# Two SBUF pools, another ring for the split branch outputs, and new transfer times in the instruction planner of a two-layer hybrid decoder

## The chip, the cores and the metric

The kernel runs on one core of a Trainium2 chip. The metric is the device time of one execution in microseconds (us), where less is better. Three runs of the kernel before gave 2449.2, 2452.07 and 2451.95 us, so the median is 2451.95 us.

A core has five engines that run their own instruction streams in order and meet through semaphores: TensorE (PE in the profile, with its weight loads shown apart as PEld), VectorE (DVE), ScalarE (ACT), GpSimd (POOL), and SyncE (SP), which here issues every transfer between HBM and SBUF.

## The reference

The reference is a trunk of two layers over 1024 tokens of width 1024, batch 1, in float32. Each layer does the following.

```python
mod = c_act @ w_ada + b_ada                    # shift, scale, gate per channel
h = rms_norm(x, norm_g) * (1.0 + scale) + shift
proj = h @ w_in                                # one projection, 8,320 columns
o_pool = causal_pool_mixer(pool_u, ...) * silu(pool_g)
o_ret  = retention(q, k, v, ...) * silu(ret_g)
o_rwkv = rwkv7_time_mix(rw, ...) * silu(rw_g)
y = einsum('btnw,nwd->btnd', branches, w_branch)
x = x + gate * (sum(sigmoid(gate_logits) * y, axis=branch) @ w_out)
```

After the second layer a final RMSNorm is applied. The pooling mixer takes trailing windows of 2 to 16 tokens, retention works in chunks of 128 tokens with 4 heads, and the RWKV-7 mixer has 8 heads of 64 with a state that is carried from token to token.

## The kernel before, in words

The activations lie transposed, channels on the 128 partitions and 512 tokens (half `h` of 0 and 1) along the free dimension. Every large product is done in `float32r` with both operands split in two, a high part that float32r holds and a low remainder, so one product of a 128x128 block takes three matmuls (`mm1`, L909): high weights with high activations, high weights with low activations, low weights with high activations. The weights are loaded in tiles of 128x512 (`wr`), and `split` (L922) makes `wh` from them on ACT and `wl` on POOL. The normed activations are `hhi` and `hlo`, 32 tiles of the ring `hb`. The outputs of the three branches go through DRAM (`od`), come back as `ol`, and are split by `split_o` (L1821) into `oG` (high) and `olo` (low); `olo` comes from the ring `mi`, eight tiles of 528 elements. The gate values, which were computed early, are kept in DRAM (`gd`) and come back into tiles of the list `gs_free` (L1841), first the seven of the ring `ri` and the four of `rk`.

The kernel does not issue its instructions where they are written. `Prog.record` (L274) notes each operation with the views it writes and reads, and gives it the priority of a running clock that the code around it keeps. `slots` (L287) gives each tile a place in its ring, `needs` (L308) finds the dependences, `cost` (L344) gives each operation a duration and a time for which it occupies its engine, and `weave` (L403) is a list scheduler: again and again it takes the engine that can start something first, and there the startable operation of the lowest priority number, until the order of every engine's stream is fixed. `give` (L458) then hands the operations to the real engines in that order, and gives each ring place its SBUF tile, all from one pool `sb`, one behind the other in the order of first use. The times of `cost` reach the chip only as this order. What an engine really waits for are the semaphores of the dependences, and an instruction whose inputs are late holds up everything behind it in its stream.

For a transfer, `cost` books 50 ns of SP and 2700 ns until it has landed, whatever else is under way; the expression in `weave` that looks at `lanes` (L424) always yields zero. VectorE and GpSimd operations with two large inputs are marked with `lock`, and `weave` does not let a locked operation of the one run beside a locked one of the other.

The program starts with the setup of layer 0 (from L1644): the eight tiles of `x` for half 0 are loaded, then the constants and the parameter vectors of layer 0 (`vec0`), four tiles of `w_ada` (into `ringG`), eight tiles of `x` for half 1, and weights. VectorE sums the squares and computes the shifts and scales in six groups (`ada`, L607) as weighted sums over `w_ada` tiles. The first large matmuls of the layer (`mms`, L1614, weights `wbig`, sums `acc6`) need the normed, shifted and split tile of each of the eight channel blocks, and the groups give the shifts of one to two blocks each. The parameter vectors of layer 1 (`vec1`) are loaded at the end of the task `rope_tables` (L694), and `derive(1)` (L695) turns them with four small VectorE operations.

Each layer then walks through its list of projection columns, with the mixers' tasks pumped in between, until ("merge",), and after it through gates, branch products and output products.

Of the kernel before, what the change touches and what calls it, by code (L numbers as in the profile page):

```python
# [10 lines left out]
F32R = mybir.dt.float32r  # L11
# [7 lines left out]
P = 128  # L19
# [239 lines left out]
class Prog:  # L259
# [14 lines left out]
    def record(self, eng, name, what, args, kw):  # L274
        o = Op()
        o.eng, o.what, o.args, o.kw = eng, (name, what), args, kw
        out = kw["out"] if "out" in kw else args[0]
        o.outs = [out]
        o.ins = [x for x in list(args) + list(kw.values()) if isinstance(x, View) and x is not out]
        o.i = len(self.ops)  # L280
        o.lane = self.lane[0]
        o.prio = self.now()
        o.pred, o.succ = {}, []
        self.ops.append(o)
        return o

    def slots(self):  # L287
        for o in self.ops:
            for x in o.outs + o.ins:
                b = x.tensor  # L290
                if b.first is None:
                    b.first = o.i
                b.last = o.i
        self.chains = {}
        used, turn = {}, {}
        for b in sorted((b for b in self.bufs if b.first is not None), key=lambda b: b.first):
            ends = used.setdefault(b.key, [])
            if len(ends) < b.bufs:
                ends.append(-1)
                k = len(ends) - 1  # L300
            else:
                k = min(range(b.bufs), key=lambda j: ends[j])
            turn[b.key] = k
            ends[k] = b.last
            b.slot = (b.key, k)
            self.chains.setdefault(b.slot, []).append(b)
# [37 lines left out]
    def cost(self, o):  # L344
        n = max((x.free_size() for x in o.outs + o.ins if x.index is not None), default=512)
        psum = any(x.space == PSUM for x in o.ins)
        wide = [x for x in o.ins if x.index is not None and x.free_size() == n and x.free_size() > 1]
        w = o.what[1]
        o.lock, o.table = False, 0
        if o.eng == "PE":  # L350
            n = o.outs[0].free_size()
            rhs = o.ins[1]
            k = rhs.index.shape[0] * 32
            if rhs.dtype == F32R:
                o.occ, o.dur = ((n + 32) / 2.4, n / 2.4 + 176) if k == 128 else (116, 393)
            elif w == "transpose":
                o.occ, o.dur = 108, 272
            elif k == 128:
                o.occ, o.dur = 222, 386 if n > 1 else 361
            else:  # L360
                o.occ, o.dur = (111, 278) if k == 64 else (64, 223)
            return
        if o.eng == "SP":
            o.occ, o.dur = 50, 2700
            return
        if o.eng == "DVE":
            if w == "reciprocal":
                d = 140 + 6.2 * n
            elif w == "transpose":
                d = 100 + 1.82 * n  # L370
            elif w == "tensor_tensor_scan":
                d = 150 + 1.7 * n
            elif w == "tensor_reduce":
                d = 150 + 1.04 * n
            elif w == "memset":
                d = 60 + 0.8 * n
            elif psum or o.outs[0].space == PSUM:
                d = 160 + 1.03 * n
            elif len(wide) > 1 or w == "tensor_tensor":
                d, o.lock = 150 + 1.05 * n, True  # L380
            else:
                d, o.lock = 150 + 0.53 * n, True
            o.dur, o.occ = d, d - 80
        elif o.eng == "ACT":
            d = (150 if psum else 185) + 0.84 * n
            if w == "activation":
                f = o.args[2] if len(o.args) > 2 else o.kw.get("func")
                o.table = SETS.get(getattr(f, "name", str(f)).split(".")[-1], 0)
                d += 100 * isinstance(o.kw.get("scale"), View) + 90 * isinstance(o.kw.get("bias"), View)
            o.dur, o.occ = d, d - 104  # L390
        else:
            if w == "memset":
                d = 100 + 0.83 * n
            elif w == "tensor_copy":
                d = 180 + 1.0 * n
            elif o.kw.get("op") == ALU.pow:
                d = 370 + 158 * n
            else:
                thin = any(0 in x.index.strides[-1:] for x in o.ins)
                d, o.lock = 190 + (1.66 if n > HF or thin else 2.12) * n, True  # L400
            o.dur, o.occ = d, d - 55

    def weave(self):  # L403
        ops = self.ops
        for o in ops:
            self.cost(o)
            o.est, o.left = 0.0, len(o.pred)
        free = {e: 0.0 for e in SPACE_LAT}
        lock = {"DVE": 0.0, "POOL": 0.0}
        ready = {e: [] for e in free}  # L410
        for o in ops:
            if not o.left:
                ready[o.eng].append(o)
        lanes, table = [0.0] * 8, 0
        order = []
        other = {"DVE": "POOL", "POOL": "DVE"}
        while len(order) < len(ops):
            best = None
            for e, q in ready.items():
                if not q:  # L420
                    continue
                f = free[e]
                if e == "SP":
                    f = max(f, lanes[len([1 for x in order if 0]) % 8])  # L424
                lk = lock[other[e]] - 100 if e in other else 0.0
                t = min(max(f, o.est, lk if o.lock else 0.0) for o in q)
                if best is None or t < best[0]:
                    best = (t, e, f, lk)
            t, e, f, lk = best
            lim = t + 1e-6 + (30 if e == "PE" else 0)  # L430
            q = ready[e]
            o = min((o for o in q if max(f, o.est, lk if o.lock else 0.0) <= lim), key=lambda o: (o.prio, o.i))
            q.remove(o)
            s = max(f, o.est, lk if o.lock else 0.0)
            d, c = o.dur, o.occ
            if o.table and o.table != table:
                d, c, table = d + 1283, c + 1283, o.table
            o.start, o.end = s, s + d
            free[e] = s + c
            if o.lock and e in lock:  # L440
                lock[e] = o.end
            order.append(o)
            for i in o.succ:
                p = ops[i]
                kind = p.pred[o.i]
                if p.eng != e or e == "SP":
                    r = o.end + SPACE_LAT[p.eng]
                elif kind == "d" and e != "PE":
                    r = o.end + SPACE_LAT[e]
                else:  # L450
                    r = s
                p.est = max(p.est, r)
                p.left -= 1
                if not p.left:
                    ready[p.eng].append(p)
        return order

    def give(self, ctx, tc):  # L458
        nc = tc.nc
        sb = ctx.enter_context(tc.tile_pool(name="sb", bufs=1))  # L460
        ps = ctx.enter_context(tc.tile_pool(name="ps", bufs=1, space=PSUM))
        dr = ctx.enter_context(tc.tile_pool(name="dr", bufs=1, space=DRAM))

        def real(b):
            if b.real is None:
                tag = "_".join(b.key) + str(b.slot[1])
                if b.space == DRAM:
                    b.real = dr.tile(b.shape, b.dtype, name=b.name)
                    return b.real
                w = HF if b.space == PSUM else self.width[b.key]  # L470
                r = (ps if b.space == PSUM else sb).tile([P, w], b.dtype, tag=tag, name=b.name)
                n = 1
                for x in b.shape[1:]:
                    n *= x
                if n != w:
                    r = r[:, 0:n]
                if len(b.shape) == 3:
                    r = r.rearrange("p (a b) -> p a b", b=b.shape[2])
                b.real = r
            return b.real  # L480
# [10 lines left out]
def trunk_kernel(ctx, tc, xT, cvec, pos, vecs, consts, w_ada, w_all, pool_w, lora_w, out):  # L491
# [1286 lines left out]
    for l in range(L):  # L1778
# [41 lines left out]

        def split_o(G, row, kt, o, h):  # L1821
            hi = G[:, kt * T + h * HF : kt * T + (h + 1) * HF].bitcast(F32R)
            lo = mi("olo").bitcast(F32R)
            split(o, hi, lo)
            row.append((hi, lo))

# [11 lines left out]
                    split_o(G, row, kt, o, h)  # L1838
                    yield 1250

        gs_free = [t_ri] * 7 + [t_rk] * 4 + [t_vp] * 2 + [t_cs] * 2  # L1841
        gs_used = {}

        def gate_tile(key):
# [232 lines left out]
```

## Time and profile before

| | |
|---|---|
| median of three runs | 2451.95 us |
| the profiled execution | 2445.24 us |
| its span | 2443.2 us |
| PE busy | 2349.6 us, 96% of the span |
| PE weight loads busy | 1903.0 us, 78% |
| VectorE, ScalarE, GpSimd busy | 1423.0, 857.1 and 845.6 us |
| transfers, mean | 92 GB/s |
| granted TensorE clock | 0.996 |

The time of an execution is slightly over its span, which runs from the first to the last recorded instruction. Matmuls are pipelined and overlap in the record, so that a busy PE is not a PE at its peak; the number of matmuls or of weight loads in a stretch says more. The windows view gives, for a stretch of time, each engine's busy time and in brackets its number of instructions. The timeline gives start, duration, engine, line, operation and tiles, with the engine's idle time before it and what ended it.

All instructions have line 487 in the profile, since `give` issues them all; they are told apart by the names of their tiles.

### The profile page before, as it was taken

What the parts mean: (1) busy time and instruction counts of PE and PEld (TensorE: products, weight loads), DVE (VectorE), ACT (ScalarE), POOL (GpSimd) and SP (SyncE); (2) the same over time, 40 slices, a digit from 0 to 9 for tenths busy, and PEclk for the clock granted to TensorE, in tenths of its full rate; (3) what the DMA queues carried; (4) which work ended last, traced back from release to release, by engine and by line L of the source; (5) the groups of instructions that cost most, each with busy time, mean ns of one, the idle gap of its engine ahead of it and who ended that gap; (6) DMA issues with size and microseconds to landing.
All of it is one profiled execution on the core that took longest, in us unless ns stands there. A gap on an engine that the chain in (4) does not pass through costs nothing. (4 is left out here: it accounts for less than half of the span.)

```text
span 2443.2 us, 33796 instructions
## 1 busy us (share of the span) xinstructions
PE 2349.6 (96%) x12520; PEld 1903.0 (78%) x12520; DVE 1423.0 (58%) x2802; ACT 857.1 (35%) x1706; POOL 845.6 (35%) x738
## 2 busy tenths in 40 slices
PE   1999999999999999998999999999999999999998
PEld 1777878878887778777887887788788778877888
DVE  4677368567657843457555845854774784412343
ACT  3642433343333232212253334334333423321343
POOL 3322233243233323364452233323323333236441
PEclk9999999999999999999999999999999999999999
DMA  6232112111213223666631211211221122454252
GB/s 218 69 90 89 44 40 71 57 44 53 82 46 94 92 70 112 211 196 199 218 109 48 87 35 44 79 42 37 66 65 37 57 99 61 128 152 144 83 149 78
DMA packets 125364, 225.68 MB, mean 92 GB/s; under 512 B 14224, under 2 KB 17552, under 8 KB 125200
## 3 DMA queue, kind: packets, MB, share of 16 engines
q1 hardware_dynamic: 125200, 223.54, 29.8%
q8 instruction: 98, 1.61, 0.3%
q14 instruction: 66, 0.54, 0.1%
HBM read 175.51 MB, written 47.97 MB: 91 GB/s over the span
## 5 line engine op out<-in xcount | busy, mean ns | idle before, releaser
L487 PE MATMUL acc<-hlo,wh 128*128 128x512 f32 x2000 | 815.1, 408 | 0.0
L487 PE MATMUL acc<-hhi,wh 128*128 128x512 f32 x2000 | 811.6, 406 | 3.2 <-DVE silu L487 2.5
L487 POOL TENSOR_TENSOR wl<-wr,wh 128x512 fp32r<-128x512 f32 x342 | 457.0, 1337 | 1028.1 <-ACT wh L487 955.6
L487 PE MATMUL acc<-hhi,wl 128*128 128x512 f32 x2000 | 811.5, 406 | 0.0
L487 PEld LDWEIGHTS acc<-hhi,wh 128*128 128x128 f32 x2000 | 377.2, 189 | 76.4 <-DVE silu L487 2.8
L487 PEld LDWEIGHTS acc<-hlo,wh 128*128 128x128 f32 x2000 | 377.4, 189 | 73.8 <-issue 3.3
L487 PEld LDWEIGHTS acc<-hhi,wl 128*128 128x128 f32 x2000 | 377.2, 189 | 73.3 <-issue 2.2
L487 ACT CAST wh<-wr 128x512 fp32r<-128x512 f32 x342 | 211.6, 619 | 622.4 <-PE acc L487 422.5
L487 PE MATMUL acc<-oG,wh 128*128 128x512 f32 x384 | 152.6, 401 | 8.5 <-ACT oG L487 6.2
L487 PE MATMUL acc<-olo,wh 128*128 128x512 f32 x384 | 153.5, 400 | 7.0 <-POOL olo L487 6.6
L487 PE MATMUL acc<-oG,wl 128*128 128x512 f32 x384 | 151.6, 395 | 0.0
L487 ACT COPY xst<-Z 64x64 f32<-64x64 f32 x256 | 62.3, 243 | 176.8 <-DVE Z L487 173.8
L487 DVE SCALAR_TENSOR_TENSOR S<-ch,pc,SP 64x64 f32<-64x64 f32 x224 | 63.4, 283 | 89.1 <-PE ch L487 80.9
L487 DVE COPY xst<-cy 64x64 f32<-64x64 f32 x256 | 55.5, 217 | 93.1 <-PE cy L487 72.2
L487 DVE TENSOR_TENSOR tm<-VB 64x30 f32<-64x30 f32 (+14 forms) x240 | 102.8, 428 | 7.6
L487 DVE TENSOR_TENSOR VB<-VB,tm 64x30 f32<-64x30 f32 (+14 forms) x240 | 98.5, 410 | 7.2
L487 DVE COPY Z<-ch 64x128 f32<-64x128 f32 x128 | 36.1, 282 | 110.4 <-PE ch L487 110.1
L487 PEld LDWEIGHTS acc<-oG,wh 128*128 128x128 f32 x384 | 72.1, 189 | 30.8 <-ACT oG L487 11.7
L487 DVE SCALAR_TENSOR_TENSOR gs<-gs,acc 128x512 f32<-128x512 f32 x64 | 43.4, 685 | 90.0 <-PE acc L487 83.0
L487 PEld LDWEIGHTS acc<-olo,wh 128*128 128x128 f32 x384 | 72.5, 189 | 26.9 <-POOL olo L487 11.4
L487 PEld LDWEIGHTS acc<-oG,wl 128*128 128x128 f32 x384 | 72.6, 189 | 16.0
L487 ACT ACTIVATE SP<-S,pc 128x128 f32<-128x128 f32 x120 | 48.2, 401 | 79.8 <-DVE S L487 79.5
(269 smaller groups left out, 3718.7 us busy)
## 6 DMA issues: line engine op xcount, KB each, us to landing
wr<-in_w_all SPq DMA_DIRECT2D x364, 256.0 KB, 2.7
gd<-gsg SPq DMA_DIRECT2D x84, 256.0 KB, 2.0
gs<-gd SPq DMA_DIRECT2D x84, 256.0 KB, 2.8
wada<-in_w_ada SPq DMA_DIRECT2D x70, 256.0 KB, 3.4
ol<-od SPq DMA_DIRECT2D x64, 256.0 KB, 3.0
ringG<-in_w_ada SPq DMA_DIRECT2D x26, 256.0 KB, 4.7
x<-in_xT SPq DMA_DIRECT2D x16, 256.0 KB, 4.8
od<-po SPq DMA_DIRECT2D x16, 256.0 KB, 2.0
```

The source lines that it names most:

```text
L487: f(*[put(x) for x in o.args], **{k: put(x) for k, x in o.kw.items()})
```

## The change

The change has five parts.

1. `record` leaves the written view out of the inputs by its place in the call, where before it left out every input that was the same view. An operation in place, such as `x = x * r`, now counts `x` as an input too; the costs and the running clock see it.
2. `slots`: where all places of a ring are still in use when a tile is first used, the place whose tile began first is taken; before, it was the one whose tile ends first.
3. The costs: a transfer occupies SP for 470 ns and takes 2650 ns, or 2100 ns where it leaves SBUF; `weave` lets no transfer land sooner than 680 ns after the one before it, and starts none before the eighth last has landed. A scan on VectorE gets the lock. A VectorE operation on PSUM costs 150 + 1.04 ns per element, or 215 + 1.0 with two full inputs, where it was 160 + 1.03.
4. `give` opens a second pool `sa`, for all tiles whose width is a multiple of 128 elements (512 bytes); the others stay in `sb`.
5. `olo` takes its tiles from `ri` (seven) and `rk` (one), 512 elements wide; the loaded gates take the eight of `mi` and three of `rk` first.

```diff
     def record(self, eng, name, what, args, kw):
-        out = kw["out"] if "out" in kw else args[0]
+        rest = [v for k, v in kw.items() if k != "out"]
+        out, rest = (kw["out"], list(args) + rest) if "out" in kw else (args[0], list(args[1:]) + rest)
         o.outs = [out]
-        o.ins = [x for x in list(args) + list(kw.values()) if isinstance(x, View) and x is not out]
+        o.ins = [x for x in rest if isinstance(x, View)]
...
-                k = min(range(b.bufs), key=lambda j: ends[j])
+                k = min(range(b.bufs), key=lambda j: ends[j] if ends[j] < b.first else b.first + began[b.key, j])
+            began[b.key, k] = b.first
...
         if o.eng == "SP":
-            o.occ, o.dur = 50, 2700
+            o.occ, o.dur = 470, 2100 if o.ins[0].space != DRAM and o.ins[0].tensor.key else 2650
...
             elif w == "tensor_tensor_scan":
-                d = 150 + 1.7 * n
+                d, o.lock = 150 + 1.7 * n, True
...
             elif psum or o.outs[0].space == PSUM:
-                d = 160 + 1.03 * n
+                d = (215 + 1.0 * n) if len(wide) > 1 else 150 + 1.04 * n
...
-        lanes, table = [0.0] * 8, 0
+        landed, table = [0.0] * 8, 0
...
                 if e == "SP":
-                    f = max(f, lanes[len([1 for x in order if 0]) % 8])
+                    f = max(f, landed[-8])
...
+            if e == "SP":
+                o.end = max(o.end, landed[-1] + 680)
+                landed.append(o.end)
...
+        sa = ctx.enter_context(tc.tile_pool(name="sa", bufs=1))
...
-                r = (ps if b.space == PSUM else sb).tile([P, w], b.dtype, tag=tag, name=b.name)
+                r = (ps if b.space == PSUM else sb if w % P else sa).tile([P, w], b.dtype, tag=tag, name=b.name)
...
-            lo = mi("olo").bitcast(F32R)
+            lo = olo_ring[olo_n[0] % 8]("olo").bitcast(F32R)
+            olo_n[0] += 1
...
-        gs_free = [t_ri] * 7 + [t_rk] * 4 + [t_vp] * 2 + [t_cs] * 2
+        olo_ring, olo_n = [t_ri] * 7 + [t_rk], [0]
+        gs_free = [mi] * 8 + [t_rk] * 3 + [t_vp] * 2 + [t_cs] * 2
```

More of the change, by code (lines that the diff above doesn't have):

```diff
@@ L294, in slots @@
         self.chains = {}
-        used, turn = {}, {}
+        used, began = {}, {}
         for b in sorted((b for b in self.bufs if b.first is not None), key=lambda b: b.first):
@@ L301, in slots @@
             else:
-                k = min(range(b.bufs), key=lambda j: ends[j])
-            turn[b.key] = k
+                k = min(range(b.bufs), key=lambda j: ends[j] if ends[j] < b.first else b.first + began[b.key, j])
+            began[b.key, k] = b.first
             ends[k] = b.last
```

## The prediction, written before the result was known

> **What bounds the kernel now.** I read the page first, then the stretches of the first 80 us, then PE's and VectorE's timelines there, and last the long stretches of large matmuls.
>
> ```profile
> span 2443.2 us, 33796 instructions
> PE 2349.6 (96%) x12520; PEld 1903.0 (78%) x12520; DVE 1423.0 (58%) x2802; ACT 857.1 (35%) x1706; POOL 845.6 (35%) x738
> ...
> PE   1999999999999999998999999999999999999998
> ...
> PE acc L487 <- POOL olo L487: 6.6, 6, 2.8
> PE acc L487 <- ACT oG L487: 6.2, 7, 1.1
> PE rot L487 <- DVE yc L487: 6.1, 6, 2.4
> ```
>
> PE is full in every slice but the first, and from 80 us on the view of PE's waits has only a few entries of some us (the three largest stand here: us in all, times, longest). From there to the end PE's own matmuls set the time. A gain must come from PE's pace or from its start, and any us that PE's full stretch begins earlier is a us of the total.
>
> The start is another matter. The columns are length, then busy time and count of PE, PEld, DVE, ACT, POOL, then clock, DMA share and GB/s.
>
> ```profile
> 5.00:10.00 5.00, 0.00 (x0) 0.00 (x0) 0.00 (x0) 2.96 (x5) 0.00 (x0) 1.00 1.01 358
> 10.00:15.00 5.00, 0.00 (x0) 0.00 (x0) 0.70 (x6) 0.00 (x0) 0.00 (x0) 1.00 1.05 395
> 15.00:20.00 5.00, 0.00 (x0) 0.00 (x0) 0.00 (x0) 0.00 (x0) 0.00 (x0) 1.00 1.06 387
> 20.00:25.00 5.00, 0.00 (x0) 0.00 (x0) 0.00 (x0) 0.00 (x0) 0.00 (x0) 1.00 1.06 388
> 25.00:30.00 5.00, 0.00 (x0) 0.00 (x0) 2.71 (x10) 0.63 (x1) 0.00 (x0) 1.00 0.39 119
> 50.00:55.00 5.00, 2.72 (x8) 2.25 (x8) 4.43 (x10) 2.66 (x4) 4.94 (x7) 1.00 0.04 14
> 70.00:80.00 10.00, 10.00 (x44) 7.94 (x43) 9.82 (x14) 9.79 (x14) 7.08 (x6) 1.00 0.24 91
> ```
>
> From 10 to 25 us the data streams in at 387 to 395 GB/s and nobody works on it. The timelines say who waits for what:
>
> ```profile
> 6.14 2.57 ACT L487 ACTIVATE sq<-x 128x512 f32<-128x512 f32 x4 [0.70 <-DMA x<-in_xT]
> ...
> 10.24 0.17 DVE L487 TENSOR_SCALAR omu<-vec 128x13 f32<-128x13 f32 x1 [9.32 <-DMA vec<-in_vecs]
> 27.29 0.17 DVE L487 TENSOR_SCALAR omu<-vec 128x13 f32<-128x13 f32 x1 [16.32 <-DMA vec<-in_vecs]
> 28.38 0.68 DVE L487 TENSOR_TENSOR sq<-sq,sq 128x512 f32<-128x512 f32 x1
> 28.98 0.48 DVE L487 SCALAR_TENSOR_TENSOR ada_ps<-ringG,cact,ada_ps 128x256 f32<-128x256 f32 x1
> 49.29 2.48 DVE L487 TENSOR_TENSOR x<-x,rbc 128x512 f32<-128x512 f32 x4 [1.34 <-ACT rbs L487]
> 79.83 0.75 DVE L487 SCALAR_TENSOR_TENSOR ada_acc<-ringG,cact,ada_ps 128x512 f32<-128x512 f32 x1
> ...
> 50.88 2.07 PE L487 MATMUL acc<-hhi,wbig 128*128 128x512 f32 x4 [2.25 <-ACT hhi L487]
> 65.04 1.22 PE L487 MATMUL acc<-hhi,wbig 128*128 128x512 f32 x2 [1.41 <-ACT rn L487]
> 69.33 2.78 PE L487 MATMUL acc<-hhi,wbig 128*128 128x512 f32 x9
> ...
> 18.31 3.72 SPq L487 DMA_DIRECT2D wada<-in_w_ada  x6
> 22.37 0.33 SPq L487 DMA_DIRECT2D vec<-in_vecs  x1
> ```
>
> The second `omu` is the first instruction of `derive(1)`, for layer 1, which nobody needs for a thousand us. It stands in VectorE's stream ahead of the sums for layer 0, and its load is issued at 22.37 us behind the six `wada`. VectorE sits 16.32 us on it, after 9.32 us on `vec0`. The old costs book every landing 2.7 us after an issue that takes 50 ns, so in the plan `vec1` is there at once and its four small operations fill a hole. PE is full from 69.33 us on.
>
> **The change part by part.**
>
> *Transfer times (SP 470 ns, 680 ns between landings).* At 388 GB/s the 262,144 bytes of a tile take 676 ns, so the plan now follows the stretch of 10 to 25 us. `vec1`, some thirtieth in the queue, lands in the plan at about 30 x 0.68 + 2.65 = 23 us or later instead of at 4, and the VectorE work that is ready before that is placed ahead of `derive(1)`. The load itself can stay where it is: behind it on SP stand only ring loads that wait for VectorE. What can fill the two holes, by what has landed (bytes summed over the stretches: all of `x` half 0 by 8.7 us, where ACT's squares end; four `ringG` tiles by 12; half 1 by 17; the next four `ringG` by 22)? Seven adds for half 0, 7 x 0.68 = 4.8; group 0, 8 x 0.48 = 3.8; four adds for half 1, 2.7; two normings of 2.48 / 4 = 0.62, 1.2; group 1, 3.8. That is 16.3 us of VectorE's work done before 27.3 us. From 27.29 to 79.83 us, where the last group ends, VectorE is busy about 43 of 52.5 us (the stretches of which three stand above, summed with the others of that view), so 16.3 us less to do brings that end forward by 16.3 x 52.5 / 43 = 20 us, and PE's full stretch with it. Bounds: at worst the later groups meet the loads for the ring instead, since its eight places are refilled only as VectorE empties them. Seven such loads take 5.6 us each to land (row below); two rounds exposed cost 11, and 20 - 11 = 9. At best VectorE stalls no more at all: the 43 - 16.3 = 27 us after 27.3 end at 54, 25 us early. I take 20.
>
> ```profile
> ringG<-in_w_ada SPq DMA_DIRECT2D x7, 256.0 KB, 5.6
> ```
>
> Elsewhere the new times cost nothing: weight tiles are loaded three ahead, a tile feeds 24 matmuls or 24 x 0.233 = 5.6 us of PE, and GpSimd, which makes the low half, sits idle before each split, so the tile waits for a free place and not the place for the tile:
>
> ```profile
> L487 POOL TENSOR_TENSOR wl<-wr,wh 128x512 fp32r<-128x512 f32 x342 | 457.0, 1337 | 1028.1 <-ACT wh L487 955.6
> ```
>
> 1028.1 / 342 = 3.0 us each. If that cover were gone, each late tile would cost what it is late beyond 3 us.
>
> *Two pools.* The compiled program before places `wh` and `wl` at 80256 and on, 384 modulo 512, and thirty of the 32 `hhi`/`hlo` tiles at 416, because tiles of odd width lie between them; two `hb` tiles and all `oG` lie at 384. With all widths in `sa` multiples of 512 bytes, all of them agree. The trace holds both cases. Four long stretches of `hhi`/`hlo` matmuls, then four of `oG`/`olo`:
>
> ```profile
> 201.60:237.98 36.38, 36.38 (x157) 29.25 (x156) 34.14 (x67) 7.12 (x13) 8.23 (x7) 1.00 0.31 95
> 1372.00:1408.36 36.36, 36.36 (x157) 29.25 (x156) 33.28 (x69) 7.74 (x14) 9.75 (x8) 1.00 0.23 73
> 1577.42:1611.47 34.05, 34.05 (x147) 27.37 (x146) 30.61 (x66) 7.82 (x15) 8.08 (x9) 1.00 0.25 77
> 2117.83:2147.43 29.60, 29.60 (x128) 23.81 (x127) 4.44 (x5) 7.93 (x15) 12.43 (x10) 1.00 0.68 215
> 2157.03:2201.32 44.29, 44.29 (x192) 35.88 (x191) 10.31 (x15) 5.47 (x9) 10.33 (x8) 1.00 0.45 127
> 2213.98:2238.85 24.87, 24.87 (x109) 20.28 (x108) 6.62 (x10) 3.11 (x5) 20.28 (x16) 1.00 0.43 123
> 1051.17:1075.75 24.58, 24.58 (x107) 19.92 (x106) 13.13 (x21) 2.76 (x5) 21.36 (x16) 1.00 0.75 230
> 1129.60:1151.47 21.87, 21.87 (x96) 17.82 (x95) 21.70 (x33) 8.10 (x14) 6.45 (x7) 1.00 0.54 157
> ```
>
> By the count of weight loads, one to a matmul, the first four take 136.39 us / 585 = 233.1 ns and the others 115.61 / 500 = 231.2 ns. The 1.9 ns are not the neighbours' doing: VectorE is near full in two of the first four and idle in the fourth, with one pace. Three groups of 2000 matmuls with `hhi`/`hlo` stand on the page, so 6000 x 1.9 = 11.6 us, all on the path, as PE is the bound. Ends: the slowest `oG` stretch, 44.29 / 191 = 231.9, gives 6000 x 1.2 = 7; the fastest, 21.87 / 95 = 230.2, gives 17. I take 12, the mean with a little for the output products. The Trainium skill speaks against this: SBUF — State Buffer, section "Who interferes with whom", gives PE two independent read ports, one for the moving operand and one for LDWEIGHTS, and says that PE never waits on anyone. By that page the addresses are worth 0 and the time is that of rival B below; these rows show two paces, if only 0.8% apart, and cannot say why.
>
> *`olo` and the gates.* The same instructions on exchanged rings, eight places for `olo` as before and fifteen for gates. The new risk is that `ri` is still held by the last RWKV outputs when the first branch's `olo` wants it. That is hidden by gate matmuls that stand ready; if the cover goes, the price is the row of POOL's burst, once per layer: 0 to 10 us each. I take 0.
>
> ```profile
> 1115.32 10.42 POOL L487 TENSOR_TENSOR olo<-ol,oG 128x512 fp32r<-128x512 f32 x7
> ```
>
> *Compute costs, inputs in place, ring places.* They issue nothing new; they move instructions. Some come nearer to the rows and one goes further off:
>
> ```profile
> L487 DVE SCALAR_TENSOR_TENSOR S<-ch,pc,SP 64x64 f32<-64x64 f32 x224 | 63.4, 283 | 89.1 <-PE ch L487 80.9
> L487 DVE COPY Z<-ch 64x128 f32<-64x128 f32 x128 | 36.1, 282 | 110.4 <-PE ch L487 110.1
> L487 DVE SCALAR_TENSOR_TENSOR gs<-gs,acc 128x512 f32<-128x512 f32 x64 | 43.4, 685 | 90.0 <-PE acc L487 83.0
> ```
>
> `S` was booked at 160 + 1.03 x 64 = 226 ns and is now 279 (row 283); `Z` goes from 292 to 283 (282); `gs`, in place, from 687 to 727 (685). PE's next step of the recurrence will meet `S` a little less early. Bounds: PE's waits after 80 us hold little more than the 19 us of the three rows above, so a gain of 15 at most, and as much again could be lost by a worse order. I take a gain of 3.
>
> **Sum.** 20 + 12 + 0 + 3 = 35 us off the profiled execution's own 2445.24 us gives 2410. That execution is 6.7 us under the median of the runs, 2451.95, so I forecast 2417 us for the runs.
>
> **The rivals.** *B, the addresses do nothing:* the paces differ for another reason, such as `oG` lying in one long tile, or the pools do not agree in the end. The two `hb` tiles at 384 speak against it only through one block in sixteen. Then 2452 - 20 - 3 = 2429. *C, the start gives back most:* VectorE is no longer held by `vec1` but by ring loads or by GpSimd, and only 9 us are won: 2452 - 9 - 12 - 3 = 2428. For it: GpSimd is 4.94 of 5 us busy at 50 us. Against: DMA is at 0.04 there, so the loads have room. *D, more is won:* 25, 17 and 10 give 2400. *E, nothing that counts:* another early filler takes `vec1`'s place and the paces stay: 2452 - 3 = 2449. *F, slower:* the scans now lock GpSimd out in the plan, its split `wl` goes behind them, the weights come late, and the next load waits on SP behind that. Place: the 16 heads of RWKV tasks. Price: all scans' time, 128 x 318 ns = 41 us, so 2452 - 35 + 41 = 2458. It decides once a split is held longer than the 3.0 us of its idle time; eight scans are 8 x 318 = 2.5 us, which speaks against.
>
> ```profile
> L487 DVE TENSOR_TENSOR_SCAN Lc<-fixed,sg 128x64 f32<-128x64 f32 x128 | 32.1, 318 | 11.6 <-ACT sg L487 10.6 <-PE nps L487 0.6
> ```
>
> **Chances and range.** Forecast 0.53, B 0.10, C 0.15, D 0.09, E 0.04, F 0.09. A measurement of this kernel can tell about 0.2%, 5 us, from no change. Faster: forecast, B, C and D, 0.87; the same: E, 0.04; slower: F, 0.09. The range, 2397 to 2444, runs from just below D to past C with a loss of 15 in the body; E and F are left out.
>
> **What would show it.** Right: no DVE idle on `vec` above 2 us in the first 30 us; the last `ada_acc` near 60 us and PE full from about 50; long `hhi` stretches at 231 ns to a weight load. Wrong: a new long idle time of VectorE at the start, `hhi` stretches still at 233, or PE's waits on `olo`, `oG` and `wl` after 80 us grown by more than 15 us.

## The result, and the profile after

The kernel after takes 2373.11 us in the median of four runs (2372.9 to 2378.03), against 2451.65 us for the kernel before (2449.2 to 2452.07). The ratio is 0.9686 with a 95% interval of 0.967 to 0.9703, so 78.5 us are gone, more than twice the 35 forecast and 24 us below the low end of the range.

The profiled execution took 2378.03 us, the slowest of the four. It is read below for where things stand, and the medians for how much they are worth. First its page: span, busy times, PE in 40 slices, granted clock, and then the three waits of PE that answer to those shown of before (us in all, times, longest), from 110 us on.

```profile
span 2376.3 us, 33823 instructions
PE 2317.6 (98%) x12520; PEld 1909.6 (80%) x12520; DVE 1428.0 (60%) x2802; ACT 858.9 (36%) x1706; POOL 842.4 (35%) x738
...
PE   4999999999999999999999999999999999999998
...
PEclk9999999999999999999999999999999999999999
...
PE acc L492 <- POOL olo L492: 6.6, 7, 2.6
PE acc L492 <- ACT oG L492: 5.2, 10, 1.0
PE rot L492 <- DVE yc L492: 1.6, 1, 1.6
```

The same 12520 matmuls are run. PE is busy for four tenths of the first slice instead of one, and the wait on `yc` has fallen from 6.1 us to 1.6, while those on `olo` and `oG` stayed.

The windows of the start, with the columns as before:

```profile
5.00:10.00 5.00, 0.00 (x0) 0.00 (x0) 2.78 (x5) 3.28 (x6) 0.00 (x0) 1.00 1.01 346
10.00:15.00 5.00, 1.87 (x8) 1.78 (x8) 4.77 (x13) 2.96 (x5) 0.00 (x0) 1.00 1.05 387
20.00:25.00 5.00, 1.71 (x8) 1.71 (x9) 4.88 (x8) 4.44 (x8) 4.94 (x6) 1.00 1.05 387
45.00:50.00 5.00, 0.12 (x1) 0.04 (x1) 4.82 (x9) 0.99 (x2) 4.30 (x4) 0.50 0.93 305
50.00:55.00 5.00, 4.48 (x11) 3.53 (x12) 4.82 (x9) 2.06 (x4) 1.28 (x1) 0.50 0.96 336
```

VectorE works while the data streams in, where it stood still before. From 45 to 55 us the granted clock of TensorE is 0.50. The timeline (start, length, engine, then in brackets the idle time before it and what ended it) shows the vectors, the last sum and PE's pauses there:

```profile
11.40 0.17 DVE L492 TENSOR_SCALAR omu<-vec 128x13 f32<-128x13 f32 x1
...
58.35 0.75 DVE L492 SCALAR_TENSOR_TENSOR ada_acc<-ringG,cact,ada_ps 128x512 f32<-128x512 f32 x1 [1.18 <-DMA ringG<-in_w_ada]
...
36.01 0.42 SPq L492 DMA_DIRECT2D vec<-in_vecs  x1
...
44.48 0.64 PE L492 MATMUL adaps<-fixed,ada_acc 128*128 128x1 f32 x4 [2.21 <-DVE ada_acc L492]
50.52 1.65 PE L492 MATMUL acc<-hlo,wbig 128*128 128x512 f32 x3 [5.39 <-DVE hlo L492]
```

No wait on `vec` is left, and the load of `vec1` has itself gone back, from 22.37 to 36.01 us. The last `ada_acc` stands at 58.35 us instead of 79.83. PE then waits once more, 5.39 us for an `hlo` that VectorE makes late, and still works at half its clock in the 5 us behind that wait. That wait keeps the clock down but did not bring it down: it begins at 45.13 us, and the window from 44.80 to 45.00 us already has a clock of 0.64, behind the pause of 2.21 us and 0.64 us of small matmuls.

Last, three long stretches of `hhi`/`hlo` matmuls and two of `oG`/`olo`:

```profile
176.10:211.46 35.36, 35.36 (x158) 29.30 (x156) 33.15 (x67) 7.64 (x13) 8.02 (x6) 1.00 0.29 90
1533.67:1562.25 28.58, 28.58 (x127) 23.66 (x126) 26.47 (x53) 7.06 (x13) 7.27 (x8) 1.00 0.23 74
2071.94:2115.03 43.09, 43.09 (x191) 35.68 (x190) 2.16 (x3) 13.49 (x23) 20.46 (x16) 1.00 0.58 177
2115.26:2158.55 43.29, 43.29 (x192) 35.88 (x191) 10.32 (x15) 5.48 (x9) 10.29 (x8) 1.00 0.47 130
2231.48:2272.34 40.86, 40.86 (x181) 33.79 (x180) 33.47 (x44) 12.76 (x21) 11.67 (x9) 1.00 0.42 125
```

To a weight load they take 107.03 us / 472 = 226.8 ns (the first three) and 84.15 / 371 = 226.8 ns (the last two). The pace of 231 ns that I took for that of agreeing operands was not it.

### The profile page after: what moved, and what is told of

Its sections match the earlier page's. It is cut to its first block, busy times and chain, and to the rows that moved or that the text cites. A ratio compares the mean times of both kernels' runs of the same rounds, so it can differ in the third digit from the quotient of the medians.

```text
span 2376.3 us, 33823 instructions
## 1 busy us (share of the span) xinstructions
PE 2317.6 (98%) x12520; PEld 1909.6 (80%) x12520; DVE 1428.0 (60%) x2802; ACT 858.9 (36%) x1706; POOL 842.4 (35%) x738
## 3 DMA queue, kind: packets, MB, share of 16 engines
q1 hardware_dynamic: 126928, 226.68, 30.7%
## 5 line engine op out<-in xcount | busy, mean ns | idle before, releaser
L492 ACT ACTIVATE gsg<-acc 128x512 f32<-128x512 f32 x90 | 53.4, 595 | 81.5 <-PE acc L492 61.8
```

Of the source, the lines that this page charges most:

```text
L492: f(*[put(x) for x in o.args], **{k: put(x) for k, x in o.kw.items()})
```

## The experiments

Theory at the outset: start and addresses as forecast, only with a larger effect of the addresses. Rivals: the new order, not the addresses, makes the pace; the planner's other parts matter more than 3 us. Each kernel was timed beside the kernel before on its chip, whose median lay between 2445.2 and 2452.1, so the ratios compare better than the times; a thousandth is 2.45 us.

| kernel | median, us | ratio | 95% interval |
|---|---|---|---|
| after | 2373.1 | 0.9686 | 0.967 to 0.9703 |
| addr_only | 2430.3 | 0.9926 | 0.9904 to 0.9949 |
| plan_only | 2392.8 | 0.9769 | 0.9754 to 0.9783 |
| off32 | 2395.2 | 0.9778 | 0.9764 to 0.9793 |
| off64 | 2379.9 | 0.9734 | 0.9715 to 0.9752 |
| off128 | 2395.1 | 0.979 | 0.9774 to 0.9805 |
| off256 | 2374.3 | 0.969 | 0.9663 to 0.9718 |
| base128 | 2381.4 | 0.972 | 0.9692 to 0.9749 |
| olo_mi | 2378.2 | 0.9696 | 0.9678 to 0.9713 |
| vec1_front | 2438.4 | 0.9946 | 0.9929 to 0.9962 |
| times_only | 2424.2 | 0.989 | 0.9864 to 0.9917 |
| t_walk | 2408.4 | 0.9836 | 0.9821 to 0.9852 |
| t_recslot | 2406.7 | 0.9828 | 0.9808 to 0.9847 |
| walk_psc | 2405.9 | 0.9832 | 0.9808 to 0.9856 |
| no_walk | 2387.1 | 0.974 | 0.9718 to 0.9761 |
| no_psc | 2384.3 | 0.9737 | 0.9722 to 0.9751 |
| no_lock | 2373.1 | 0.9694 | 0.9679 to 0.971 |
| g_low | 2371.8 | 0.9692 | 0.9677 to 0.9707 |

### The addresses alone, and everything but the addresses

addr_only is the kernel before with the two pools and the exchanged rings; plan_only is the kernel after without them.

```diff
+        sa = ctx.enter_context(tc.tile_pool(name="sa", bufs=1))
...
-    ... else sb).tile(
+    ... else sb if w % P else sa).tile(
...
-            lo = mi("olo").bitcast(F32R)
+            lo = olo_ring[olo_n[0] % 8]("olo").bitcast(F32R)
```

> The kernel before with the two pools and the exchanged rings alone; its instruction order is the old plan's. Theory 1 (the agreement of addresses sets PE's pace, and a stretch must agree throughout for some ten matmuls before it reaches 226.7 ns): long stretches of large matmuls at 226.7 ns to a weight load, for hhi as for oG, the start as before (VectorE 16 us idle on the vectors, PE full from 69 us), about 40 to 45 us faster, 2407 to 2412 us. Theory 2 (the new order is what made PE faster, the addresses only 2 ns): stretches at 231 ns, 2438 to 2442 us.

> The changed kernel with one pool and olo back in the ring mi; only the planner's parts are left. The one pool is filled in the order of first use, so the offsets between operands are mixed. Theory 1: stretches at 231 to 233 ns, PE full from about 50 us, 20 to 25 us faster than before, 2427 to 2432 us. Theory 2: stretches at 227 to 229 ns and 2385 to 2400 us.

The planner's parts are worth about 57 us (0.9769) and the addresses about 20, whether put on the kernel before (0.9926, 18 us) or taken off the kernel after (0.9769 against 0.9686). As the stretches below show, each run has the pace of Theory 1, but addr_only has the time of neither theory, and plan_only has that of Theory 2. In plan_only, with mixed offsets, 36.10 / 156 = 231.4 ns stand in this stretch:

```profile
176.60:212.70 36.10, 36.10 (x157) 29.31 (x156) 33.24 (x67) 8.12 (x14) 8.72 (x7) 1.00 0.27 89
```

In addr_only, in the old order, the stretches have the new pace:

```profile
200.46:235.82 35.36, 35.36 (x158) 29.28 (x156) 33.26 (x67) 7.02 (x12) 7.94 (x6) 1.00 0.30 97
2144.76:2188.05 43.29, 43.29 (x192) 35.85 (x191) 10.30 (x15) 5.47 (x9) 10.30 (x8) 1.00 0.47 129
```

35.36 / 156 = 226.7 ns, so the order is not what makes the pace. But 233.1 - 226.7 = 6.4 ns on the 6000 matmuls of the page's three large groups would be 38 us, and half of it is missing. The starts in the two traces say where most of it is: between adjoining large matmuls less than 300 ns apart (6072 pairs in before, 6044 in addr_only) the mean distance falls from 232.6 to 228.1 ns, by 4.5 ns instead of 6.4, which is 27 us. The 6.4 ns hold only deep in a long stretch, and a third of these pairs are among the first seven of theirs. With the pairs that are further apart, the large matmuls together gain 22 us (1642 to 1620), and the pauses take some of that back. The longest of them in the body shows in the timeline of addr_only and in its windows:

```profile
976.29 0.39 PE L488 MATMUL acc<-olo,wh 128*128 128x512 f32 x1
980.53 1.09 PE L488 MATMUL rot<-cst,yc 128*128 128x128 f32 x4 [3.85 <-DVE yc L488]
981.27 0.78 PE L488 MATMUL acc<-oG,wl 128*128 128x512 f32 x1
981.84 0.63 PE L488 MATMUL acc<-oG,wh 128*128 128x512 f32 x1
982.27 0.63 PE L488 MATMUL acc<-olo,wh 128*128 128x512 f32 x1
...
978.00:980.00 2.00, 0.00 (x0) 0.00 (x0) 1.36 (x1) 0.17 (x2) 1.83 (x2) 0.80 0.73 252
980.00:985.00 5.00, 4.47 (x17) 4.02 (x17) 1.13 (x2) 1.02 (x2) 1.27 (x1) 0.50 0.45 126
985.00:990.00 5.00, 5.00 (x15) 3.98 (x15) 2.45 (x4) 0.33 (x2) 1.29 (x1) 0.56 0.82 293
```

A faster PE comes sooner to a step of the retention mixer that is not ready. It waits 3.85 us for `yc`, and its clock falls to 0.50: starts of large matmuls are 0.43 us apart (981.84 to 982.27). At a clock of 0.50 and 0.56 the ten microseconds, of which the first 0.5 us are still the pause, hold 4.7 us less than at full clock. The Trainium skill, TensorE: Matmul & The Clock Gate, Part 1, lets the clock fall to half after an idle window of about 3.4 us. The fall came sooner here: PE's last matmul ends at 976.68 us, and a mean of 0.80 from 978 to 980 us puts the fall to 0.50 at about 979.2, 2.5 us later. In the kernel before a pause of 2.35 us was enough:

```profile
811.43 1.12 PE L487 MATMUL rot<-cst,yc 128*128 128x128 f32 x4 [2.35 <-DVE yc L487]
...
812.00:814.00 2.00, 2.00 (x7) 1.67 (x6) 1.35 (x4) 0.00 (x0) 0.00 (x0) 0.50 0.11 33
```

Over the body the windows view shows longer pauses too, for before and then for addr_only:

```profile
110.00:2100.00 1990.00, 1959.32 (x10621) 1579.04 (x10620) 1250.83 (x2508) 699.82 (x1437) 663.48 (x582) 1.00 0.27 83
```

```profile
110.00:2100.00 1990.00, 1952.98 (x10679) 1592.14 (x10678) 1265.62 (x2519) 703.28 (x1447) 665.51 (x584) 0.99 0.27 84
```

1990 less PE's time is 30.7 us of idle before and 37.0 in addr_only. 22 us less these 6.3 is about the 16 us by which the two profiled executions differ (2445.24 and 2429.24 us).

### Which agreement counts

off32, off64, off128 and off256 are the kernel after with the ring `hb` (`hhi`, `hlo`, `mhi`, `mlo`) moved by so many bytes against the weights; the order of the instructions is the same. base128 opens the two pools in the other order, so that both operands lie at 128 modulo 512. olo_mi gives `olo` its old ring back.

The diff, with its long line wrapped, is that of off256, where four tiles of an odd width (each shifts what follows by 64 bytes) go into a pool of their own; off128 has two and off64 one, and off32 has a smaller tile there.

```diff
-    r = (ps if b.space == PSUM else sb if w % P else sa).tile(
+    r = (ps if b.space == PSUM else gap if b.key[-1] == "mo" and b.slot[1] < 4
+         else sb if w % P else sh if b.key[0] == "hb" else sa).tile(
```

> The changed kernel, with the tiles of hhi, hlo, mhi and mlo moved 32 bytes against the weights (480 and 448 modulo 512), which is the offset of the kernel before; oG and olo still agree with the weights. The order of instructions is that of the changed kernel. Theory 1: hhi stretches at 233 ns, oG stretches at 226.7 ns, 30 to 40 us slower than the changed kernel, 2403 to 2413 us. Theory 2: 2373 us.

> The kernel after with hhi, hlo, mhi and mlo moved by 64 bytes against the weights. At 32 bytes of difference a matmul took 233.3 ns and the kernel 2395.2 us, at 256 bytes 226.9 ns and 2374.3 us, at 384 to 416 against each other 233.1. Theory A (the operands must agree modulo 256): 233 ns, 2392 to 2398. Theory B (modulo 64 is enough): 226.9 ns, 2371 to 2377.

> The kernel after with hhi, hlo, mhi and mlo moved by 128 bytes against the weights. Theory A (agreement modulo 256 needed): 233 ns, 2392 to 2398. Theory B (modulo 64 or 128 is enough): 226.9 ns, 2371 to 2377.

> The changed kernel with hhi, hlo, mhi and mlo moved 256 bytes against the weights modulo 512 (480 and 224). Theory 1 as the change states it (modulo 512): hhi stretches at 231 to 234 ns, 2403 to 2413 us. Rival (the agreement that counts is modulo 256 or less): 226.7 ns and 2373 us.

> The changed kernel with the two pools in the other order, so that all large operands lie at 128 modulo 512 instead of 480, and still agree. Theory 1: no difference, 226.7 ns and 2373 us within 4. Theory 3 (what counts is where the operands lie, not that they agree): another pace, 231 ns or more, and 2400 us or more.

> The changed kernel with olo back in the ring mi, so that one of three matmuls in the oG stretches has an operand that does not agree (seven of its eight places), while hhi and hlo agree with the weights throughout. Theory 1 (a stretch must agree throughout): hhi stretches stay at 226.7 ns, oG stretches fall back to 230 to 232 ns in all three of their matmuls, so 1152 x 4.5 ns = 5 us slower, 2378 us. Rival (each matmul pays for itself alone): only olo's 384 pay 6 ns, oG stretches at 228.7 ns, 2 us slower.

The same stretch in off32, off64, off128 and off256, one fence for each:

```profile
176.54:212.94 36.40, 36.40 (x158) 29.23 (x156) 33.31 (x67) 8.15 (x14) 8.92 (x7) 1.00 0.27 88
```

```profile
175.56:211.27 35.71, 35.71 (x157) 29.30 (x156) 33.23 (x67) 7.88 (x14) 8.46 (x7) 1.00 0.27 89
1532.90:1562.30 29.40, 29.40 (x128) 23.81 (x126) 26.88 (x53) 7.06 (x13) 7.29 (x8) 1.00 0.25 72
```

```profile
176.92:213.32 36.40, 36.40 (x157) 29.28 (x156) 33.57 (x67) 8.14 (x14) 8.47 (x7) 1.00 0.28 88
```

```profile
175.76:211.12 35.36, 35.36 (x158) 29.28 (x156) 33.15 (x67) 7.64 (x13) 8.13 (x6) 1.00 0.27 90
```

To a weight load: 233.3 ns at 32 bytes, 228.9 at 64 (but 29.40 / 126 = 233.3 in another stretch), 233.3 at 128, and 226.7 at 256 as at 0. The expectations of off64 and off128 asked whether agreement modulo 256 is needed (Theory A) or less is enough (B): off128 came out as A, and neither had the value in between that off64 shows. Agreement modulo 512, which the change makes, is more than is needed: modulo 256 was enough. By the ratio 64 bytes cost about 12 us (0.9734), half of what 32 or 128 cost; why, I can't explain. base128 kept 226.9 ns, so the place itself does not count. Its ratio is 0.0034 above that of the kernel after, with intervals that overlap; its four runs took 2388.5, 2381.4, 2381.4 and 2372.1 us at a granted clock of 0.985, 0.988, 0.988 and 0.994, so the excess goes with the clock. off32 against the kernel after, 0.9778 - 0.9686, is 22 us for one offset and nothing else: the addresses do it. In olo_mi two of three matmuls of an `oG` stretch have agreeing operands, and yet:

```profile
175.79:211.15 35.36, 35.36 (x158) 29.29 (x156) 33.15 (x67) 7.64 (x13) 8.06 (x6) 1.00 0.29 90
2112.08:2156.49 44.41, 44.41 (x193) 35.84 (x191) 10.31 (x15) 5.46 (x9) 10.34 (x8) 1.00 0.45 127
```

44.41 / 191 = 232.5 ns for the whole stretch, against 226.7 for the `hhi` stretch above it. One misaligned operand in three spoils nearly all of it. That fits the 231.2 ns in the rows of before: their `oG` stretches had `olo` in eight places of which one agreed. The pools and the exchange of `olo` are one step, not two.

### The start

times_only is the kernel before with the new transfer times alone. vec1_front is the kernel before with the load of `vec1` right behind that of `vec0`, and nothing else.

```diff
     nc.sync.dma_start(out=vec[0], in_=vecs[0])
+    nc.sync.dma_start(out=vec[1], in_=vecs[1])
```

> The kernel before with the transfer times alone (470 ns, 2650 or 2100 ns, 680 ns apart, eight under way), none of the other planner's changes and one pool. If these times are the cause of the earlier start: PE full from about 50 us, 2428 to 2436 us. If the other cost changes are needed for it: PE full later than 60 us, 2440 us or more. The offsets between operands are mixed, as in the run with the planner's parts alone.

> The kernel before with one edit: the load of vec1 is issued right behind that of vec0. If the 16 us of VectorE's idle time on it were the whole of the start, PE is full from about 50 us and the time falls by 15 to 20 us, 2432 to 2437 us. If VectorE's old order only meets the next late tile instead, the gain is under 8 us, 2444 us or more. The addresses shift as well; by the offsets (160 modulo 512 for hhi) the pace stays at 231 to 234 ns.

The last groups' `ada_acc` (count, durations, from the first to the last) in times_only and in vec1_front:

```profile
L490 DVE SCALAR_TENSOR_TENSOR ada_acc<-ringG,cact,ada_ps x3: 481/747/748, 42.1 to 57.8; 128x512 f32<-128x512 f32 x2, 128x256 f32<-128x256 f32 x1
```

```profile
L487 DVE SCALAR_TENSOR_TENSOR ada_acc<-ringG,cact,ada_ps x3: 482/741/748, 46.9 to 67.9; 128x512 f32<-128x512 f32 x2, 128x256 f32<-128x256 f32 x1
```

The last one moves from 79.83 us to 57.8 with the transfer times alone, 22 us, and times_only is 27 us faster (0.989; the interval reaches from 20 to 33), 4 us below the time expected. Some 4 of these us are pace: the places in the one pool move too, and the mean distance of adjoining large matmuls falls from 232.6 to 231.9 ns. Taking away only VectorE's wait on `vec1` brings the last `ada_acc` to 67.9, 12 us, and 13 us of time (0.9946), between the two times expected. At 110 us PE has worked 58.3 us in before, 70.5 in vec1_front and 82.4 in times_only. So that wait was about half of the start's gain, and the rest is what the true landing times do for the order of the other loads and sums.

### The planner's other parts

From times_only (0.989) to plan_only (0.9769) 30 us are open, where I had booked 3. What I had not followed: the code that walks through the columns also keeps a clock, and `settle` (L727), which advances the engines and tiles of that clock, reads the inputs that `record` notes. With inputs in place it sees that chains of operations in place end later, lets the mixers' tasks go on later, and computes more gate columns early meanwhile. The transfers show it, in before and in plan_only:

```profile
gd<-gsg SPq DMA_DIRECT2D x84, 256.0 KB, 2.0
```

```profile
gd<-gsg SPq DMA_DIRECT2D x90, 256.0 KB, 2.0
```

Four kernels take this apart. t_walk is times_only with the new ring rule, and the inputs in place seen by the walk alone; no_walk is the kernel after with the walk's clock as before; no_psc has the old cost of VectorE operations on PSUM, no_lock no lock for scans.

In t_walk the inputs without those in place are kept in `plan_ins`, and the planner takes them once the walk is over; in no_walk they are kept in `walk_ins`, and `settle` takes these. The four edits, in this order:

```diff
     def slots(self):
+        for o in self.ops:
+            o.ins = o.plan_ins
...
-            ins, outs = o.ins, o.outs
+            ins, outs = o.walk_ins, o.outs
...
-                d = (215 + 1.0 * n) if len(wide) > 1 else 150 + 1.04 * n
+                d = 160 + 1.03 * n
...
-                d, o.lock = 150 + 1.7 * n, True
+                d = 150 + 1.7 * n
```

> The kernel before with the new transfer times, the new rule for ring places, and the changed record seen by the running clock alone: the planner's costs and dependences still leave inputs in place out. So the walk through the columns is that of the kernel after (90 gate halves are stored early instead of 84), and the order inside is planned with the old costs. With the transfer times alone the kernel took 2424.2 us, with all the planner's parts 2392.8, so 31 us are open. Theory W (the walk: VectorE's chains in place are now seen to be late, so the pumping of the RWKV tasks leaves PE more other work between their steps): 2395 to 2402, and PE's waits on yc at rot fall from 8.7 us to under 2. Theory P (the planned order: costs of in-place operations, PSUM costs, the lock of the scans): 2420 to 2428, waits as before. Theory M (a little of each): 2405 to 2415.

> The kernel after, but the running clock that steers the walk leaves inputs in place out, as in the kernel before (84 gate halves early); planner, pools and rings are those of the kernel after. The kernel after took 2373.1 us. Theory W: 2395 to 2405, most of the 31 us is lost. Theory P: 2370 to 2378. Theory M: 2380 to 2390.

> The kernel after with the old cost of VectorE operations on PSUM (160 + 1.03 ns per element, whatever the inputs). Theory W: within 4 us of the kernel after (2369 to 2377), the order changes in many places but PE remains full. Theory P, if these costs carry it: 2390 to 2405.

> The kernel after without the lock that the planner now sets for scans. Theory W: within 4 us of the kernel after (2369 to 2377). Theory P, if the lock carries it: 2385 to 2405. My rival F (the lock holds the split of the weights back) would make this one faster than the kernel after, by more than 5 us.

The walk is worth 13 us on the one side (0.989 to 0.9836, with the ring rule, which was not run alone) and 13 on the other (0.974 against 0.9686). Theory W asked for twice that; the numbers are M's, a part from the walk and a part from the planned order. W's mechanism is there, in the wait on `yc` of times_only, then of t_walk, and, with the walk taken out of the kernel after (1.6 us there), of no_walk:

```profile
PE rot L490 <- DVE yc L490: 8.7, 7, 2.6
```

```profile
PE rot L494 <- DVE yc L494: 1.6, 1, 1.6
```

```profile
PE rot L493 <- DVE yc L493: 4.8, 4, 2.3
```

The PSUM costs are worth 12 us when taken out of the kernel after (0.9737), and the lock nothing that can be told (0.9694). Whether walk and PSUM costs add up was asked of two more: walk_psc adds the PSUM costs to t_walk, t_recslot adds to it the inputs in place in the planner's costs instead.

> The kernel with the new transfer times, ring rule and walk (2408.4 us), and the new costs of VectorE operations on PSUM beside them; the planner's own costs and dependences still leave inputs in place out. The kernel with all the planner's parts took 2392.8 us, and taking the PSUM costs out of the kernel after cost 11.2 us. If the parts add up: 2396 to 2400. If the PSUM costs only help together with the in-place inputs in the planner: 2405 to 2410.

> The kernel before with the new transfer times, the new rule for ring places and the whole changed record (the walk and the planner's costs and dependences see inputs in place), with the old costs on PSUM and no lock. The same without the planner's share took 2408.4 us, all the planner's parts together 2392.8. If the in-place inputs in the planner's costs carry the rest by themselves: 2393 to 2397. If they help only together with the PSUM costs: 2402 to 2409.

Neither gives more than t_walk that could be told (0.9832 and 0.9828 against 0.9836), and both together, with the lock that counts for nothing, give 0.9769. So the planner's costs carry another 16 us, but only with both parts in; one alone leaves an order as bad. The code couples the two: the new price of 215 + 1.0 ns is for two full inputs, and a sum in place on PSUM such as `ada_ps` with 256 columns has two only once its input in place counts. It is booked at 424 ns before, 416 with the PSUM costs alone, 424 with the inputs in place alone and 471 with both; the profile has 480. That these sums make the better order was not tested. PE's body in times_only, t_walk, walk_psc, t_recslot and plan_only:

```profile
110.00:2100.00 1990.00, 1957.95 (x10641) 1584.27 (x10640) 1245.35 (x2494) 698.76 (x1438) 671.32 (x585) 0.99 0.27 85
```

```profile
110.00:2100.00 1990.00, 1964.99 (x10698) 1594.64 (x10697) 1249.82 (x2496) 700.52 (x1443) 669.88 (x588) 0.99 0.28 86
```

```profile
110.00:2100.00 1990.00, 1967.41 (x10711) 1598.96 (x10711) 1250.05 (x2496) 702.05 (x1443) 667.40 (x588) 0.99 0.28 86
```

```profile
110.00:2100.00 1990.00, 1967.30 (x10716) 1597.08 (x10715) 1239.92 (x2497) 705.02 (x1444) 668.10 (x588) 1.00 0.28 86
```

```profile
110.00:2100.00 1990.00, 1976.48 (x10769) 1607.31 (x10768) 1248.56 (x2498) 707.26 (x1451) 671.92 (x591) 1.00 0.28 87
```

Idle time falls in the same steps as the ratios: 32.1, 25.0, 22.6, 22.7 and 13.5 us. That is 18.5 of the 30 us. The other 11 are not idle in the record: by the pages PE is busy for 2349.4 us in times_only and 2338.0 in plan_only, at the same mean clock (0.993). By the starts no group of matmuls of one kind takes more than 3.3 us less, so they are spread thin; the cause stays open. A part of them may be the slower matmuls after each pause.

### A try at more

g_low lets GpSimd make the `hlo` for which PE waited 5.39 us.

```diff
-    low(V, 1, 0)
+    low(G_, 1, 0)
```

> The kernel after, with the low half of half 1's first block made by GpSimd instead of VectorE, where it stands behind fourteen steps of the ada groups (49.78 us) though its input is there from about 41 us. PE then should not sit idle for 5.39 us before it, and its clock should not fall to 0.50 from 45 to 55 us. If both count: 4 to 8 us less than the kernel after (2365 to 2369). If PE only waits for the next ada group instead: the same, 2371 to 2376.

The ratio of 0.9692 is that of the kernel after, the second of the two outcomes expected. The wait went to the next thing that is late, 4.42 us on an ada group, and the clock fell to 0.50 in the next window all the same:

```profile
50.39 0.56 PE L492 MATMUL adaps<-fixed,ada_acc 128*128 128x1 f32 x2 [4.42 <-DVE ada_acc L492]
...
50.00:55.00 5.00, 3.26 (x8) 2.65 (x9) 4.82 (x8) 4.03 (x6) 2.84 (x3) 0.50 0.97 361
```

No kernel tried beats the kernel after.

## Why the prediction was wrong

*The start, 20 us: right.* The signs named came: no idle time on `vec`, the last `ada_acc` near 60 us (58.35), PE full from about 50 (50.52). By the last `ada_acc` it is 21.5 us, by times_only 27 with an interval that holds 20 and some 4 us of pace in it. That `vec1` was the cause of the whole is only half right, by vec1_front. Not foreseen were the move of `vec1`'s load, which I had left in its place, and the 5.39 us wait at half clock. In the queue of before `vec1` stands thirty-seventh, not some thirtieth; by the same sum it then lands at 28 us in the plan, which changes nothing in the argument.

*Two pools, 12 us: mechanism right, size off.* It measured about 20, above the upper bound of 17. The step that failed is the price of 1.9 ns. I took 231.2 ns for the pace of agreeing operands, from where `oG` lies and without a word on where `olo` lies; the compiled program had it agree in one place of eight. That pace is 226.8. The whole 6.3 ns, 38 us, would have been as wrong on the other side, since the step lets all of it lie on the path: about half did not arrive. By addr_only, 11 us of it were never there, since the mean over all adjoining pairs falls by 4.5 ns and not by 6.4, and most of the rest went into 6.3 us of longer idle time and the clock that falls behind it (4.7 us at one place). Rival B falls with off32. So does, for this case, what I concluded from the Trainium skill, SBUF — State Buffer, "Who interferes with whom", which gives PE two independent read ports and lets it wait on no one: that the addresses are worth nothing. A difference of 32 bytes between moving and weight addresses costs 22 us; by what mechanism, no run here shows.

*Exchange of `olo` and gates, 0: right on the waits, wrong on the pace.* The waits on `olo` stayed (6.6 us). Without the exchange the `oG` stretches go at 232.5 ns; on the page's 3 x 384 matmuls that would be 6.6 us; olo_mi's median is 5.1 us longer, by the ratios 2.5, with intervals that overlap.

*Compute costs, inputs in place, ring places, 3 us: the term that failed most.* It measured 30, and with it the sum failed. The sentence "They issue nothing new; they move instructions" was wrong: the walk's clock reads the same record, and six more gate halves go through DRAM. And the bound of 15, from the largest three waits of PE, left out that a better order also shortens the many small ones. F, that the lock would hold the splits back, falls with no_lock.

*The sum.* Along the chain times_only, t_walk, plan_only, after the ratios give 27 us for the transfer times, 13 for the walk, 16 for the planner's costs and 20 for the addresses: 77 us, 0.0314 of 2451.65. D, at 2400, went in the right direction, but its bounds of 17 and 10 were too low, and without the walk no bound of the body could have been right.

## What to carry to other kernels

When a recorded quantity is changed, find every reader of it before costing the change: here one line fed a scheduler and, through a clock, the choice of what is computed early. A pace read as "the aligned case" has to be checked for every operand in it, since here one in three spoiled the stretch. And where PE is full, a gain of pace and the waits behind it belong together: price the next wait, and the clock that falls with it, before counting matmuls times nanoseconds.

## What the runs showed of the hardware

A `float32r` matmul of 128x512 in a long stretch took 226.8 ns where its moving operand and its weights agreed modulo 256 bytes (after, off256), 233.3 at 32 bytes of difference (off32) and in the stretch shown at 128 (off128), and mostly 228.9 at 64 (off64). Behind a pause or matmuls of another kind the faster pace comes only after some matmuls: by the starts in the trace of the kernel after, the median distance is 231 to 233 ns for the first three pairs of a series of large matmuls and 227 from the seventh on. And in addr_only a pause of PE of 3.85 us cost about as much again in the clock that fell with it, 4.7 us; in the kernel before a pause of 2.35 us was followed by a clock of 0.50.
